# First 256 tokens multiplied before their row factors are known, and their scaled parts written again later

## The chip, the cores and the metric

The kernel runs on one core of a Trainium2 chip. The metric is device time in microseconds (us) of one launch, as a median over several runs. The engines are PE (TensorE, matrix products, with PEld for its weight loads), DVE (VectorE), ACT (ScalarE), POOL (GpSimd) and SP (SyncE, which here only issues DMA transfers). PE accumulates in PSUM, everything else lies in SBUF or in DRAM.

## What is computed

Two sequences of 512 tokens go through one encoder layer. Only its beginning matters here:

```python
def rms_norm(x, g):
    xf = x.astype(jnp.float32)
    y = xf * lax.rsqrt(jnp.mean(xf * xf, axis=-1, keepdims=True) + EPS)
    return (y * g.astype(jnp.float32)).astype(x.dtype)
...
h = rms_norm(x, ln1)
proj = h @ w_in
q, k, v, u, g_att, g_ssm = jnp.split(proj, IN_SPLITS, axis=-1)
...
dt = jnp.exp(log_dt.astype(jnp.float32))[..., None]
mag = jnp.exp(lr * dt)
ang = li * dt
```

Each token's row is divided by its root mean square (the row factor) and multiplied by the gain `ln1` of each column; then come the projections. `u` feeds a state-space branch whose coefficients need `dt`, `mag`, `ang` and powers of the complex number they make. Since a row factor is one number per token, it may as well be applied behind the product: (f x) W = f (x W).

## The kernel before

**Products.** The tokens stand in columns: `xT` is x turned, in eight pieces (k = 0 to 7) of 128 model columns. A float32 product is made of three of a shorter type: each operand is split into a high part (`hi`, a cast on ACT) and a low part (`lo`, what the cast left over, a subtraction on DVE or POOL), and PE adds hi*hi, hi*lo and lo*hi (in code p = 0, 1 and 2, where p == 2 takes the low part of the weights and p == 1 that of the tokens). `hT[s]` holds the two parts of the normalized, turned tokens of sequence s (in the profile `act` for s = 0, `hT` for s = 1). They are used by all projections.

**The opening.** It is written out by hand: PE, ACT, DVE and SP take their instructions in the order of the code there; POOL's order is the scheduler's. The first three columns of `u` (128 outputs each; weights `uw` for c = 0, 1 and `c_hi`, `c_lo` for c = 2) are multiplied while the inputs arrive:

- SP issues row blocks 0 to 3 of `x` (`xt`, 128 tokens x 1024, 512 KB each), then the columns of `xT` (`xc`, 512 tokens, 256 KB each) and the weights in halves of 256 KB, then rows and columns of sequence 2, then small things. A buffer that is used again holds its transfer back until its readers are done, and all transfers behind it.
- `row_root(t)`: ACT squares a row block and sums along the row (L355), POOL adds EPS and takes the power -1/2 (L357, L358).
- `spread(s, t)`: DVE puts the 128 factors on a diagonal (L348), PE multiplies it by ones (L349), so that a PSUM bank holds the factors of the tokens along its columns, the same in every partition.
- `scaled(s, k)`: DVE multiplies a column by gain and factor (L364, `rn_xn`), ACT casts it (L365), DVE or POOL subtracts (L368, L367; POOL for odd k).
- L383 is a warm-up of PE, on row block 2 and ones. L463 are the products, nine for each k (three columns, three parts), 512 tokens wide, first of sequence 1 into `tps`, `tps`, `sps`, then of sequence 2 into `sps`, `acc`, `po`.
- `exp_exact`, an exponential of 15 small DVE instructions on 128x64, runs twice at the very start (L326 to L338), for `dt` and `mag`; the angle follows in pieces during sequence 2.

**Behind it** `u_steps(3)` and `u_steps(4)` are queued in `fill` as 16 steps of three products each (L115 to L117), which `run(n)` puts between the other work; they use the parts of both sequences. Meanwhile DVE makes the powers of the complex number (`pr`, `pi`: `first_power`, L413 to L418, then L479 to L484), ACT copies them (L489 to L493), and DVE makes coefficients (L537 to L549) and tables (L561 to L573: `bpre` and `ctab`, for 16 quads of groups in turn). `bpre` has one buffer: PE's turns (L596) of one quad need its `bpre`, and DVE starts the next quad's `bpre` when they are done. Later a scan over chunks runs on DVE, beside products on PE.

Of the kernel before, what the change touches and what calls it, by code (L numbers as in the profile page):

```python
# [18 lines left out]
P = 128  # L19
D = 1024  # L20
# [43 lines left out]
def hybrid_layer(ctx, tc, x, xT, rel, onehot, early, w_qkv, w_ug, q_gain, k_gain, sink,  # L64
# [165 lines left out]
    def u_steps(c):  # L230
        up, ps = [], {}

        def out(s):
            S.copy(up[0][:, :, s, :], ps[s].rearrange("p (k t) -> p t k", t=T))
            if s:
                u_store(c, up[0])

        def step(s, k):
            if s + k == 0:
                up.append(evp.tile([P, T, NSEQ, NCHUNK], F32, tag="ev", name="up"))  # L240
# [3 lines left out]
            if k == KT - 1:  # L244
                act_owed.append(lambda: out(s))
                if s:
# [25 lines left out]
    with tc.tile_pool(name="xin", bufs=2, reuse_waits="tile") as xin, tc.tile_pool(name="ssmc", bufs=1) as sc:  # L272
# [10 lines left out]
        rows, columns, first_w = {}, {}, []  # L283

        def x_rows(s):
            for t in range(s * 4, s * 4 + 4):
                rows[t] = xin.tile([P, D], F32, tag="xt", name="xt", bufs=4)
                SP.dma_start(rows[t], x[t * P:(t + 1) * P, :])

        def x_columns(s, k0=0, k1=KT):  # L290
            for k in range(k0, k1):
                columns[s, k] = xin.tile([P, HALF], F32, tag="xc", name="xc", bufs=8)
                SP.dma_start(columns[s, k], xT[k, :, s * HALF:(s + 1) * HALF])
# [19 lines left out]
        second = cast_owed[:]  # L313
        del cast_owed[:]
        bc_tiles = {0: b_and_c(0)}
        SP.dma_start(dd[32:48, :], d_skip)
        SP.dma_start(bglu_sb, b_glu)
# [5 lines left out]
        def exp_exact(dst, src):  # L323

            n, r, q = c64("ex_n"), c64("ex_r"), c64("ex_q")
            V.tensor_scalar(r, src, -87.0, 88.5, op0=ALU.max, op1=ALU.min)  # L326
            V.tensor_scalar(n, r, 1.0 / math.log(2.0), ROUND_MAGIC, op0=ALU.mult, op1=ALU.add)
            V.tensor_scalar_add(n, n, -ROUND_MAGIC)
            V.scalar_tensor_tensor(r, n, -LN2_HI, r, op0=ALU.mult, op1=ALU.add)
            V.scalar_tensor_tensor(r, n, -LN2_LO, r, op0=ALU.mult, op1=ALU.add)  # L330
            V.tensor_scalar(q, r, 1.0 / 5040.0, 1.0 / 720.0, op0=ALU.mult, op1=ALU.add)
            V.tensor_mul(q, q, r)
            for cf in (1.0 / 120.0, 1.0 / 24.0, 1.0 / 6.0, 0.5, 1.0):
                V.scalar_tensor_tensor(q, q, cf, r, op0=ALU.add, op1=ALU.mult)
            V.tensor_scalar_add(q, q, 1.0)
            bits = sc.tile([P, GROUPS], I32, tag="ex_i", name="ex_i")
            V.tensor_scalar(bits, n, 127.0, 8388608.0, op0=ALU.add, op1=ALU.mult)
            V.tensor_mul(dst, q, bits.bitcast(F32))  # L338
# [3 lines left out]

        def spread(s, t):

            if t == 0:
                spread_ps[s] = acc()
# [4 lines left out]
        def row_root(t):  # L351

            junk = xin.tile([P, D], F32, tag="rn_junk", name="rn_junk", bufs=1)
            ss = small.tile([P, 1], F32, tag="ss", name="ss")
            S.activation(junk, rows[t], AF.Square, scale=D ** -0.5, accum_out=ss)  # L355
# [4 lines left out]
        def scaled(s, k):  # L360

            xn = xin.tile([P, HALF], F32, tag="rn_xn", name="rn_xn", bufs=3)
            hi, lo = [q[:, k, :] for q in hT[s]]
            V.scalar_tensor_tensor(xn, columns[s, k], ln1_sb[:, k:k + 1], spread_ps[s], op0=ALU.mult, op1=ALU.mult)  # L364
# [5 lines left out]
        def weight_half(raw, w, i):  # L370
            sl = slice(i * KT // 2, (i + 1) * KT // 2)
            S.copy(w[0][:, sl, :], raw[:, sl, :])
            return lambda: V.tensor_sub(w[1][:, sl, :], raw[:, sl, :], w[0][:, sl, :].bitcast(F32))

        exp_exact(dt, ldt)
        for t in range(4):
            row_root(t)
        w_los = [weight_half(raw, w, 0) for raw, w in first_w]
        V.tensor_mul(mag, lr, dt)
        exp_exact(mag, mag)  # L380
        warm = acc()
        for i in range(6):
            PE.matmul(warm[:, 0:P], rows[2][:, 0:P], ones, start=True, stop=True)  # L383

        for t in range(4):
            spread(0, t)
        w_los.pop(0)()
        owed = [scaled(0, 0)]
        second.pop(0)()
        w_los.append(dve_owed.pop())  # L390
# [4 lines left out]
        def u_out(c, s):  # L395
            S.copy(ups[c][:, :, s, :], out_ps[c, s].rearrange("p (k t) -> p t k", t=T))

        def angles():
            yield lambda: V.tensor_mul(ang, li, dt)
# [5 lines left out]
            yield lambda: None  # L405
# [1736 lines left out]
```

## Time and profile before

| | us |
|---|---|
| median of 3 runs | 1452.25 (1452.12 to 1452.64) |
| the profiled execution | 1451.68 |
| its span, first to last instruction | 1449.9 |
| PE busy in the span | 1431.1 (99%) |
| DVE, ACT, POOL busy | 1083.6, 770.8, 190.9 |

How to read its lines: those of the page's fifth part and of the groups give line, engine, operation, output<-inputs, shapes and count, then busy us and mean ns, then idle time ahead and what ended it. Those of a timeline give the start, the us from start to end (of several merged ones where x2 and more stands), and the same names. Matmul records overlap: a 128x512 product has 0.39 us in them, but the next starts 0.227 us later. Those of windows give the busy us of PE, PEld, DVE, ACT and POOL in a stretch, PE's granted clock, the DMA share and GB/s.

### The profile page before, as it was taken

What the parts mean: (1) busy time and instruction counts of PE and PEld (TensorE: products, weight loads), DVE (VectorE), ACT (ScalarE), POOL (GpSimd) and SP (SyncE); (2) the same over time, 40 slices, a digit from 0 to 9 for tenths busy, and PEclk for the clock granted to TensorE, in tenths of its full rate; (3) what the DMA queues carried; (4) which work ended last, traced back from release to release, by engine and by line L of the source; (5) the groups of instructions that cost most, each with busy time, mean ns of one, the idle gap of its engine ahead of it and who ended that gap; (6) DMA issues with size and microseconds to landing.
All of it is one profiled execution on the core that took longest, in us unless ns stands there. A gap on an engine that the chain in (4) does not pass through costs nothing.

```text
span 1449.9 us, 21455 instructions
## 1 busy us (share of the span) xinstructions
PE 1431.1 (99%) x7718; PEld 1225.6 (85%) x7718; DVE 1083.6 (75%) x1842; ACT 770.8 (53%) x1393; POOL 190.9 (13%) x267
## 2 busy tenths in 40 slices
PE   6999999999999999999999999999999999999998
PEld 5888888888999999988888888888888888888887
DVE  7899979974536999987764798777776588475644
ACT  5589962224426999896432455554555444333332
POOL 4111120000222555372001000000000000000000
PEclk9999999999999999999999999999999999999999
DMA  8355568259941433455862335544443994464341
GB/s 304 112 162 173 169 195 284 95 172 287 297 131 44 128 100 110 135 190 167 269 215 95 107 103 188 183 143 141 152 149 121 327 343 127 155 194 144 127 131 58
DMA packets 130134, 243.86 MB, mean 168 GB/s; under 512 B 16059, under 2 KB 59323, under 8 KB 130028
## 3 DMA queue, kind: packets, MB, share of 16 engines
q1 hardware_dynamic: 105740, 187.39, 41.2%
q10 hardware_dynamic: 21888, 46.15, 8.4%
q0 software_dynamic: 2400, 8.95, 1.8%
q8 instruction: 61, 1.00, 0.3%
q14 instruction: 45, 0.37, 0.1%
HBM read 173.20 MB, written 81.82 MB: 176 GB/s over the span
## 4 chain that ended last, share of the span: by engine, by line
PE 94%; DVE 2%; DMA 1%; ACT 1%; issue 1%; POOL 1%; SPq 0%; DVEq 0%; ACTq 0%
PE bank L115 14%; PE bank L117 14%; PE bank L116 14%; PE acc L141 12%; PE acc L732 9%; PE acc L770 5%; PE acc L115 3%; PE acc L117 3%; PE acc L116 3%; PE po L1103 3%; PE sps L1071 2%; PE tps L1087 2%; PE sps L605 2%; PE sps L877 2%; PE lag L620 1%; PE tps L596 1%
## 5 line engine op out<-in xcount | busy, mean ns | idle before, releaser
L117 PE MATMUL bank<-b_hi,a_lo 128*128 128x512 f32 x440 | 171.2, 389 | 0.0
L116 PE MATMUL bank<-b_lo,a_hi 128*128 128x512 f32 x440 | 171.2, 389 | 0.0
L115 PE MATMUL bank<-b_hi,a_hi 128*128 128x512 f32 x440 | 171.2, 389 | 0.0
L2015 ACT CAST a_hi<-d_a 128x1024 fp32r<-128x1024 f32 x55 | 57.8, 1051 | 178.7 <-PE bank L116 175.5
L2016 DVE TENSOR_TENSOR a_lo<-d_a,a_hi 128x1024 fp32r<-128x1024 f32 x55 | 67.4, 1225 | 98.8 <-ACT a_hi L2015 96.7
L117 PE MATMUL bank<-act,u_lo 128*128 128x512 f32 x256 | 99.6, 389 | 0.0
L116 PE MATMUL bank<-act,u_hi 128*128 128x512 f32 x256 | 99.6, 389 | 0.0
L115 PE MATMUL bank<-act,u_hi 128*128 128x512 f32 x256 | 99.6, 389 | 0.0
L117 PEld LDWEIGHTS bank<-b_hi,a_lo 128*128 128x128 f32 x440 | 82.6, 188 | 17.3
L116 PEld LDWEIGHTS bank<-b_lo,a_hi 128*128 128x128 f32 x440 | 82.6, 188 | 17.2
L115 PEld LDWEIGHTS bank<-b_hi,a_hi 128*128 128x128 f32 x440 | 82.6, 188 | 17.0
L732 PE MATMUL acc<-w_hi,hT 128*128 128x256 f32 x384 | 84.4, 293 | 0.0
L732 PE MATMUL acc<-w_hi,act 128*128 128x256 f32 x384 | 81.2, 290 | 0.0
L141 PE MATMUL acc<-act,c_hi 128*128 128x512 f32 x256 | 80.6, 395 | 0.0
L141 PE MATMUL acc<-hT,c_hi 128*128 128x512 f32 x256 | 80.5, 394 | 0.0
L1081 ACT ACTIVATE p<-p,nmx 128x257 f32<-128x257 f32 (+1 forms) x128 | 72.0, 564 | 13.0 <-DVE nmx L1075 12.3
L1075 DVE CUSTOM_DVE_ANT_0 p<-sps,bias,nsink 128x256 f32<-128x256 f32 (+1 forms) x128 | 69.3, 542 | 4.4 <-PE sps L1071 3.0
L1799 ACT CAST u_hi<-s 128x512 fp32r<-128x512 f32 x64 | 39.3, 621 | 59.6 <-PE bank L116 36.2
L2016 DVE TENSOR_TENSOR b_lo<-k,b_hi 128x1024 fp32r<-128x1024 f32 x55 | 67.1, 1220 | 0.0
L732 PEld LDWEIGHTS acc<-w_hi,hT 128*128 128x128 f32 x384 | 63.8, 190 | 0.9
L732 PEld LDWEIGHTS acc<-w_hi,act 128*128 128x128 f32 x384 | 63.1, 190 | 0.8
L1096 DVE TENSOR_TENSOR pl<-tps,ph 128x512 fp32r<-128x512 f32 x80 | 55.0, 688 | 4.5 <-ACT ph L1091 2.7
(407 smaller groups left out, 3939.0 us busy)
## 6 DMA issues: line engine op xcount, KB each, us to landing
d_a<-a_scr SPq DMA_DIRECT2D x55, 512.0 KB, 3.6
u_raw<-in_w_up_dram SPq DMA_DIRECT2D x32, 512.0 KB, 5.8
a_scr<-t ACTq DMA_DIRECT2D x64, 256.0 KB, 2.1
k<-in_w_down_dram SPq DMA_DIRECT2D x32, 512.0 KB, 6.1
a_scr<-a ACTq DMA_DIRECT2D x48, 256.0 KB, 3.3
c_raw<-in_w_ug_dram SPq DMA_DIRECT2D x44, 256.0 KB, 3.5
ct_scr<-ctab SPq DMA_DIRECT2D x16, 576.0 KB, 3.3
ctab_in<-ct_scr SPq DMA_DIRECT2D x32, 288.0 KB, 4.8
```

Of the source, the lines that this page charges most:

```text
L115: PE.matmul(ps, a[0], b[0], start=first, stop=False)
L116: PE.matmul(ps, a[0], b[1], start=False, stop=False)
L117: PE.matmul(ps, a[1], b[0], start=False, stop=last)
L141: PE.matmul(self.ps[s], self.w[p == 2][:, k, :], hT[s][p == 1][:, k, :], start=i % (3 * KT) == 0, stop=i % (3 * KT) == 3 * KT - 1)
L732: PE.matmul(ps, act[p == 2][:, k, col:col + P], self.w[k // 4][p == 1][:, k % 4, :], start=i == 0, stop=i == 3 * KT - 1)
L770: PE.matmul(self.ps[s], w_g[self.m][p == 2][:, k, :], y_part(s, int(p == 1), k), start=k + p == 0, stop=k == KT - 1 and p == 2)
L1075: V.tensor_tensor_reduce(self.p[:, h, 1:1 + self.nk], self.s[h][:, 0:self.nk], biases[self.j][h][:, b0:b0 + self.nk], -1.0, nsink[:, hh:hh ...
L1081: S.activation(p, p, AF.Exp, bias=self.nmx[:, h:h + 1], scale=-1.0, accum_out=self.sums[:, h, self.qb:self.qb + 1])
L1096: V.tensor_sub(pl, self.pt[i], self.hl[i][0].bitcast(F32))
L1103: PE.matmul(self.po, vv, self.hl[i][part], start=i + part == 0, stop=i == self.nkb - 1 and part == 1)
L2015: S.copy(hi, src)
L2016: V.tensor_sub(lo, src, hi.bitcast(F32))
```

## The change

Only the opening is changed; all instructions from the power tables on are the same, on each engine in the same order.

- The first 256 tokens of sequence 1 are split without their factors: `raw_parts` (ACT: gain times column, as it is cast; DVE: gain times column less the high part). Their products, 256 wide, start with the first columns and weights. The factor is applied when the PSUM bank is evacuated: `u_scaled_out` multiplies by `factor` on DVE (three times, during sequence 2).
- The other 256 tokens are scaled as before, 256 wide, in a second pass over k. Of the row blocks, 2 and 3 are therefore loaded first, 4 to 7 then, and 0 and 1 last.
- The parts of the first 256 tokens are needed with their factors by every later product. Their columns are loaded once more (`x_again`, 1 MB) and `rewrite(k)` writes the parts anew; `u_steps(3)` takes sequence 2 first.
- The two exponentials are dealt out, one to three instructions at a time (`some`), over the opening. The warm-up multiplies ones by ones. The squares overwrite their rows instead of a junk tile. `column_in(3)` moves ahead.

**PE, the first products.** Before (L383 is the warm-up, L349 the spreads of the factors, L463 the products; `act_113` and `act_114` are the high and the low parts of sequence 1):

```order
L383 MATMUL acc<-ones,xt 128x128 x6
L349 MATMUL acc<-rs_diag,ones 128x128 x4
L463 MATMUL tps<-act_113,uw_hi 128x512 x2
L463 MATMUL sps<-act_113,c_hi 128x512
L463 MATMUL tps<-act_113,uw_lo 128x512 x2
```

Now, on the same engine (L465 is the warm-up, L443 the products):

```order
L465 MATMUL acc<-ones 128x128 x6
L443 MATMUL tps<-act_113,uw_hi 128x256
L443 MATMUL tps<-act_114,uw_hi 128x256
L443 MATMUL tps<-act_113,uw_lo 128x256
L443 MATMUL tps<-act_113,uw_hi 128x256
```

The spreads have gone from the front; two of them now stand ahead of the second 256 tokens, four among that part's last products, and two in sequence 2.

**ACT, the second 256 tokens** (L417 are the casts of the scaled columns, L400 the squares of row blocks 4 to 7). Now:

```order
L417 CAST act_113<-rn_xn 128x256 x3
L400 ACTIVATE xt,ss<-xt 128x1024
L417 CAST act_113<-rn_xn 128x256
L400 ACTIVATE xt,ss<-xt 128x1024
L417 CAST act_113<-rn_xn 128x256
L400 ACTIVATE xt,ss<-xt 128x1024
L417 CAST act_113<-rn_xn 128x256
L400 ACTIVATE xt,ss<-xt 128x1024
L417 CAST act_113<-rn_xn 128x256 x2
```

A square of a row block stands ahead of each cast from k = 3 on; before they stood so among the casts of k = 4 to 7 of all 512 tokens.

**DVE, ahead of the power tables.** Before (L221 is the low part of weights, L418 the first power's last instruction, L479 the first of the tables):

```order
L221 TENSOR_TENSOR c_lo<-c_raw,c_hi 128x512
L413 MEMSET pr 128x64
L414 MEMSET pi 128x64
L415 TENSOR_TENSOR sh<-sh 128x64
L416 TENSOR_SCALAR sh<-sh 128x64
L417 TENSOR_TENSOR pr<-mag,sh 128x64
L418 TENSOR_TENSOR pi<-mag,sn 128x64
L479 TENSOR_TENSOR tm_640<-pr 128x64
```

Now, between the same first power and the same first table (L415 and L420 are the columns written anew and their low parts):

```order
L459 TENSOR_TENSOR pi<-mag,sn 128x64
L221 TENSOR_TENSOR c_lo<-c_raw,c_hi 128x512
L415 SCALAR_TENSOR_TENSOR rn_xn<-xa,early_sb,acc 128x256 x3
L420 TENSOR_TENSOR act_114<-rn_xn,act_113 128x256
L1018 TENSOR_SCALAR nsink<-nsink 128x16
L415 SCALAR_TENSOR_TENSOR rn_xn<-xa,early_sb,acc 128x256 x2
L420 TENSOR_TENSOR act_114<-rn_xn,act_113 128x256
L415 SCALAR_TENSOR_TENSOR rn_xn<-xa,early_sb,acc 128x256 x2
L420 TENSOR_TENSOR act_114<-rn_xn,act_113 128x256
L415 SCALAR_TENSOR_TENSOR rn_xn<-xa,early_sb,acc 128x256
L420 TENSOR_TENSOR act_114<-rn_xn,act_113 128x256
L566 TENSOR_TENSOR tm_769<-pr 128x64
```

Twelve instructions have come in ahead of the power tables. The other four low parts are POOL's.

The diff, cut to what the text speaks of:

```diff
-    def u_steps(c):
+    def u_steps(c, order=(0, 1)):
...
-        return [lambda s=s, k=k: step(s, k) for s in range(NSEQ) for k in range(KT)]
+        return [lambda s=s, k=k: step(s, k) for s in order for k in range(KT)]
...
-        x_rows(0)
-        x_columns(0, 0, 1)
+        x_half(0, 0)
         first_weights(0)
-        column_in(2)
-        x_columns(0, 1, 4)
+        third_weights(0)
+        for k in range(1, 4):
+            x_half(k, 0)
+        x_row(2)
         first_weights(1)
-        x_columns(0, 4, KT)
-        x_rows(1)
-        x_columns(1)
+        third_weights(1)
+        for k in range(4, KT):
+            x_half(k, 0)
+        x_row(3)
+        for k in range(KT):
+            x_half(k, 1)
+        for t in range(4, 8):
+            x_row(t)
+        for k in range(4):
+            x_column(k)
+        for t in range(2):
+            x_row(t)
+        for k in range(4, KT):
+            x_column(k)
         bc_tiles = {0: b_and_c(0)}
         SP.dma_start(dd[32:48, :], d_skip)
+        column_in(3)
+        for i in range(2):
+            x_again(i)
...
+        def raw_parts(k):
+            hi, lo = [q[:, k, 0:H2] for q in hT[0]]
+            src, gain = columns[0, k][:, 0:H2], ln1_sb[:, k:k + 1]
+            S.activation(hi, src, AF.Copy, scale=gain)
+            return lambda: V.scalar_tensor_tensor(lo, src, gain, hi.bitcast(F32), op0=ALU.mult, op1=ALU.subtract)
...
+        def u_scaled_out(c):
+            V.tensor_tensor(ups[c][:, :, 0, 0:H2 // T], out_ps[c, 0][:, 0:H2].rearrange("p (k t) -> p t k", t=T),
+                            factor.rearrange("p (k t) -> p t k", t=T), op=ALU.mult)
...
+        in_turn = {0: ((1, 2), (1, 2)), 1: ((3, KT), (3,)), 2: ((KT + 1, 4), (KT, 4)), 3: ((KT + 2, 5), (KT + 1, KT + 2)),
+                   4: ((6,), (5,)), 5: ((7,), (6,)), 6: ((), (7,)), 7: ((), ())}
+        for k in range(KT):
+            if k == 1:
+                halves(3)
+                row_root(2)
+                halves(KT)
+            else:
+                halves(*in_turn[k][0])
+            if k == 5:
+                row_root(3)
+            low_parts(*in_turn[k][1])
+            if k > 3:
+                some(3)
+            u_products(0, k, 0, H2, by_part if k else by_column)
+        for t in (2, 3):
+            spread(0, t)
+        low = scaled(0, 0, H2, HALF)
+        for k in range(KT):
+            after = scaled(0, k + 1, H2, HALF) if k + 1 < KT else None
+            low()
+            low = after
+            if 0 < k < 5:
+                row_root(k + 3)
+            some(1)
+            u_products(0, k, H2, HALF, by_part, slice(0, 6 if k == KT - 1 else 9))
...
+            if k == 2:
+                for t in range(2):
+                    spread(0, t)
+                factor = xin.tile([P, H2], F32, name="factor", bufs=1)
+                S.copy(factor, spread_ps[0][:, 0:H2])
         column_in(4)
-        fill += u_steps(3)
+        fill += u_steps(3, (1, 0))
         fill += u_steps(4)
         run(2)
-        for c in range(3):
-            u_out(c, 1)
-            u_store(c, ups[c])
+        for k in range(2, KT):
+            rewrite(k)
+            rewritten.pop(0)()
+            if k < 5:
+                u_out(k - 2, 1)
+                u_store(k - 2, ups[k - 2])
+        for fn in rewritten:
+            fn()
```

More of the change, by code (lines that the diff above doesn't have):

```diff
@@ L338, in exp_exact @@
-            V.tensor_mul(dst, q, bits.bitcast(F32))
+            yield lambda: V.tensor_scalar(bits, n, 127.0, 8388608.0, op0=ALU.add, op1=ALU.mult)
+            yield lambda: V.tensor_mul(dst, q, bits.bitcast(F32))
         dt, mag, ang, kk = c64("dt"), c64("mag"), c64("ang"), c64("kk")
         spread_ps, root = {}, {}
-        def spread(s, t):
-            if t == 0:
-                spread_ps[s] = acc()
-            dg = xin.tile([P, P], F32, tag="rs_diag", name="rs_diag", bufs=4)
-            V.tensor_scalar_mul(dg, ident, root[s * 4 + t])
-            PE.matmul(spread_ps[s][:, t * P:(t + 1) * P], ones, dg, start=True, stop=True)
@@ L351, in row_root @@
[L351 to L355, printed above, removed]
-            root[t] = small.tile([P, 1], F32, tag="rs", name="rs")
-            GP.tensor_scalar_add(ss, ss, EPS)
-            GP.tensor_tensor(root[t], ss, neg_half[:, 0:1], op=ALU.pow)
[L360 to L364, printed above, removed]
-            S.copy(hi, xn)
-            if k % 2:
-                return lambda: GP.tensor_tensor(lo, xn, hi.bitcast(F32), op=ALU.subtract)
-            return lambda: V.tensor_sub(lo, xn, hi.bitcast(F32))
@@ L370, in weight_half @@
[L370 to L390, printed above, removed]
-        u_w = [w for raw, w in first_w] + [weights[2]]
-        out_ps = {}
-        ups = [xin.tile([P, T, NSEQ, NCHUNK], F32, tag="up", name="up", bufs=3) for c in range(3)]
-        def u_out(c, s):
-            S.copy(ups[c][:, :, s, :], out_ps[c, s].rearrange("p (k t) -> p t k", t=T))
         def angles():
+            yield from exp_exact(dt, ldt)
@@ L404, in angles, with some, spread @@
             yield lambda: V.tensor_scalar(ang, ang, -3.1415925, 3.1415925, op0=ALU.max, op1=ALU.min)
-            yield lambda: None
         small_ops = angles()
+        def some(n):
+            for _ in range(n):
+                next(small_ops, nop)()
+        def spread(s, t):
+            dg = xin.tile([P, P], F32, tag="rs_diag", name="rs_diag", bufs=4)
+            V.tensor_scalar_mul(dg, ident, root[s * 4 + t])
+            PE.matmul(spread_ps[s][:, t * P:(t + 1) * P], ones, dg, start=True, stop=True)
@@ L465, in hybrid_layer, with halves @@
-        for fn in w_los:
-            fn()
+        warm = acc()
+        spread_ps[1] = acc()
+        spread_ps[0] = acc()
+        for i in range(6):
+            PE.matmul(warm[:, 0:P], ones, ones, start=True, stop=True)
+        for c in range(3):
+            out_ps[c, 0] = (tps, tps, sps)[c]()
+        some(4)
+        raw_parts(0)()
+        for c in range(3):
+            weight_half(c, 0)()
+        lo = {}
+        def halves(*names):
+            for n in names:
+                lo[n] = raw_parts(n) if n < KT else weight_half(n - KT, 1)
@@ new lines, in hybrid_layer, with rewrite @@
+        low = scaled(1, 0)
+        for c in range(3):
+            out_ps[c, 1] = (sps, acc, lambda: ps_o.tile([P, 512], F32, tag="po", name="po"))[c]()
+        rewritten = []
+        def rewrite(k):
+            rewritten.append(scaled(0, k, 0, H2, columns["again", k]))
+        for k in range(KT):
+            after = scaled(1, k + 1) if k + 1 < KT else None
+            low()
+            low = after
+            if k < 3:
+                u_out(k, 0, H2, HALF)
+            if k < 2:
+                row_root(k)
+            if k in (3, 4, 5):
+                u_scaled_out(k - 3)
+            some(3)
+            if k == 4:
+                S.activation(sn, ang, AF.Sin)
+                S.activation(sh, ang, AF.Sin, scale=0.5)
+            if k == 6:
+                first_power()
+            if k in (3, 5):
+                pay(cast_owed, 1)
+            if k in (4, 6):
+                pay(dve_owed)
+            if k > 5:
+                rewrite(k - 6)
+            u_products(1, k, 0, HALF, by_part)
+            if k == 2:
[3 more added lines that the diff above has]
+                S.copy(factor, spread_ps[0][:, 0:H2])
```

145 lines of the change are left out of this document (77 added, 68 removed).

## Prediction

> **What bounds the kernel now.** I read the page first, then the waits of PE (TensorE), then the timelines of the opening. The page's first lines, its slices and its chain:
>
> ```profile
> span 1449.9 us, 21455 instructions
> PE 1431.1 (99%) x7718; PEld 1225.6 (85%) x7718; DVE 1083.6 (75%) x1842; ACT 770.8 (53%) x1393; POOL 190.9 (13%) x267
> PE   6999999999999999999999999999999999999998
> PE 94%; DVE 2%; DMA 1%; ACT 1%; issue 1%; POOL 1%; SPq 0%; DVEq 0%; ACTq 0%
> ```
>
> PE is busy everywhere but in the first slice of 36 us, so a change in the opening pays what it takes from PE's idle time there, if PE's head start lives through the stages behind. PE's waits and its timeline (start, us, what; the product of interest is L463):
>
> ```profile
> PE acc L383 <- DVE ex_q L331: 8.0, 1, 8.0
> PE tps L463 <- ACT act L365: 1.5, 1, 1.5
> PE acc L349 <- DVE rs_diag L348: 1.2, 2, 0.7
> PE sps L463 <- DVE c_lo L221: 0.7, 1, 0.7
> 8.04 2.90 PE L383 MATMUL acc<-ones,xt 128*128 128x128 f32 x12 [8.04 <-DVE ex_q L331]
> 14.13 0.73 PE L463 MATMUL tps<-act,uw_hi 128*128 128x512 f32 x2 [1.49 <-ACT act L365]
> 27.95 0.60 PE L349 MATMUL acc<-rs_diag,ones 128*128 128x128 f32 x4
> 34.72 0.39 PE L463 MATMUL sps<-hT,uw_hi 128*128 128x512 f32 x1
> 51.04 0.39 PE L115 MATMUL acc<-act,c_hi 128*128 128x512 f32 x1
> ```
>
> The first product starts at 14.13, the second sequence's first at 34.72, and the next stage at 51.04. The second sequence (72 products, 16.3 us) has no gap, so all that can be won lies before 34.72, where 72 products of 0.227 us (51.04 - 34.72 over 72) need only 16.3 us.
>
> **The first product.** The loads land in the order of issue, one behind another:
>
> ```profile
> 2.73 0.20 DVE L326 TENSOR_SCALAR ex_r<-early_sb 128x64 f32<-128x64 f32 x1 [0.91 <-DMA early_sb<-in_early_dram]
> 5.35 1.06 ACT L355 ACTIVATE rn_junk<-xt 128x1024 f32<-128x1024 f32 x1 [3.35 <-DMA xt<-in_x_dram]
> 6.69 1.06 ACT L355 ACTIVATE rn_junk<-xt 128x1024 f32<-128x1024 f32 x1 [0.19 <-DMA xt<-in_x_dram]
> ```
>
> 512 KB are there at 5.35, the next 512 KB 1.3 us later. Now 384 KB stand ahead of the first product (half a column of x, half a weight column): 5.35 less a quarter of 1.3, so 5.0, and a weight cast of 0.62 (below) makes **5.7**. Bounds: 4.5, if short loads land as the first small one did (read at 2.73); 6.0, if 384 KB take as long as 512 KB did.
>
> **First half of sequence 1 (256 tokens).** Of products on 256 columns the trace has this stretch, first and last row of nine products (ends left out), and of the other operations these rows (mean ns behind the bar):
>
> ```profile
> 371.97 0.40 PE L732 MATMUL acc<-w_hi,act 128*128 128x256 f32 x2
> ...
> 372.92 0.28 PE L732 MATMUL acc<-w_lo,act 128*128 128x256 f32 x1
> L364 DVE SCALAR_TENSOR_TENSOR rn_xn<-xc,early_sb,acc 128x512 f32<-128x512 f32 x16 | 11.6, 738 | 1.1 <-PE acc L349 0.9 <-DMA xc<-in_xT_dram 0.2
> L372 ACT CAST uw_hi<-uw_raw 128x512 fp32r<-128x512 f32 x4 | 2.5, 618 | 1.1 <-DMA uw_raw<-in_w_ug_dram 0.9
> L373 DVE TENSOR_TENSOR uw_lo<-uw_raw,uw_hi 128x512 fp32r<-128x512 f32 x4 | 2.7, 682 | 0.0
> L367 POOL TENSOR_TENSOR hT<-rn_xn,hT 128x512 fp32r<-128x512 f32 x4 | 5.2, 1309 | 10.4 <-ACT hT L365 10.4
> L358 POOL TENSOR_TENSOR rs<-ss,neg_half 128x1 f32<-128x1 f32 x8 | 4.6, 569 | 0.7
> L334 DVE SCALAR_TENSOR_TENSOR ex_q<-ex_q,ex_r 128x64 f32<-128x64 f32 x10 | 2.3, 225 | 0.3
> L355 ACT ACTIVATION_READ_ACCUMULATOR rn_junk<-xt 128x1 f32 x8 | 1.5, 186 | 0.0
> L357 POOL TENSOR_SCALAR ss<-ss 128x1 f32<-128x1 f32 x8 | 2.7, 332 | 8.1 <-DVE mag L379 5.3 <-ACT rn_junk L355 2.6
> L512 ACT COPY a8s<-pr 128x256 f32<-128x256 f32 x1 | 0.4, 405 | 0.0
> L479 DVE TENSOR_TENSOR tm<-pr 128x256 f32<-128x256 f32 x1 | 0.4, 427 | 0.0
> ```
>
> Eight products start between 371.97 and 372.92: 0.119 us each, so 72 take 8.6 us (two halves cost 0.8 us more than 16.3). PE would end at 14.3, but k = 4 needs the second weight halves. Ahead of the last of them 2.5 MB are queued (row block 2 among them): 5.35 + 4 x 1.3 = 10.5. Its cast (0.62) and subtraction (0.68), with the other two subtractions and k = 4's own low part on DVE, put it at about 12.9; the 30 products behind it take 3.6 us: **16.7**. The exponentials' small steps (225 ns each, twelve between here and the diagonals) fill DVE so that the diagonals come some 0.4 us after PE is done.
>
> **The factors for the second half.** Two diagonals and spreads (1.0 us with that wait), then the scaled column and its cast, 256 wide. The trace has neither; they lie between half and all of 738 and 618 ns, and I take 0.46 and 0.41, by the two 128x256 rows. First product of the second half: **18.6**.
>
> **Second half.** 8.6 us of products and four spreads (1.0). ACT has eight casts (0.41) and four squares (1.06 and a readout of 0.19): 8.3 us. POOL has four subtractions and four roots: at 0.7 each (half of 1309; bounds 0.65 and 1.31) and 0.33 + 0.57, 6.4 us. Neither is longer than PE, but they are in line: a cast stands behind the square of its turn, a subtraction behind a root. I put 1.3 us of waits for that (nothing if they run ahead, 3 us at POOL's upper bound). End **29.7**; then 0.74 and 0.62 for the first column of sequence 2: **31.1**, 3.6 us before 34.72.
>
> **Sequence 2** is as before, but for the two spreads of the early tokens (0.5 us on PE) and a subtraction on POOL that comes 0.2 us late. The next stage starts 2.9 us earlier than 51.04. I take off 0.3 us for PE's slow start: the warm-up's twelve records took 2.90 us, four of the spreads at 27.95 only 0.60 us: 0.21 us apart (2.90 less the last one's 0.4, over twelve) and 0.11 (0.60 less 0.27, over three). The same 128x128 operation costs half as much once PE has run for a while. The warm-up now waits for a memset alone, ends near 3.7 and leaves PE idle until 5.7. At half speed, 0.21 apart, the 36 products up to k = 3 would end at 13.3, against the weights' 12.9: 0.4 us if it lasts so long, nothing if it ends sooner. **PE's head start: 2.6 us.**
>
> [...]
>
> **What DVE, ACT and DMA do with it.** The parts written anew add eight columns to DVE and ACT just ahead of the power tables:
>
> ```profile
> 44.41 0.11 DVE L413 MEMSET pr<- 128x64 f32 x1
> 46.22 0.22 DVE L479 TENSOR_TENSOR tm<-pr 128x64 f32<-128x64 f32 x1
> 51.28 0.42 DVE L484 TENSOR_TENSOR pi<-tm,tm 128x256 f32<-128x256 f32 x1
> 53.27 0.63 ACT L489 COPY e<-pr 64x512 f32<-64x512 f32 x1
> 68.70 1.29 DVE L221 TENSOR_TENSOR c_lo<-c_raw,c_hi 128x512 fp32r<-128x512 f32 x2 [0.81 <-ACT c_hi L220]
> 73.88 1.23 DVE L561 TENSOR_TENSOR bpre<-b,bk 128x1024 f32<-128x1024 f32 x1 [3.89 <-PE tps L596]
> 85.50 1.23 DVE L573 TENSOR_TENSOR bpre<-bpre,tb 128x1024 f32<-128x1024 f32 x1
> 89.05 1.03 PE L596 MATMUL tps<-ident,bpre 128*128 128x128 f32 x8
> 40.00:45.00 5.00, 5.00 (x24) 4.14 (x23) 4.01 (x9) 3.86 (x7) 2.05 (x2) 1.00 0.17 52
> ```
>
> In sequence 2 DVE waits for the factor: PE has the spreads at 31.1 + 6.1 + 0.5, ACT copies it by 38.4; all of DVE's queue stands behind (the columns from k = 5 on, the evacuations), which brings the memset of pr to about 44.7 (44.41 before): the exponentials' steps here and the three scaled evacuations eat DVE's part of the head start. Then come eight columns (0.39 apart), four subtractions (0.35), and some 1.6 us of waits for ACT's casts and POOL: 6.2 us. The power tables end at about 58 instead of 51.7. ACT's copies start right then, not 1.6 us after as before (53.27), so they are 4.9 us late, and with them the tables of the first quad. DVE's idle 0.81 and 3.89 us take up 4.7 of that. So DVE starts the second quad's bpre at 73.9 plus 0 to 1 us; I take **0.5 us later than now**, where PE is 2.6 us earlier. The bounds are 1.5 us later (POOL's and DVE's upper ends) and 0.8 us earlier (all at half of the 512-wide rows).
>
> From 73.88 on DVE has hardly a gap, and PE's third turn at 89.05 comes 2.3 us after its bpre (85.50 + 1.23). So PE keeps at most 2.3 - 0.5 = **1.8 us**, and waits 0.8 us there. Behind that both run as before, the same instructions in the same order, and PE's slices show no room to lose or win it.
>
> At no cost: the junk tile that goes (same squares), the columns read again (1 MB, landing near 35, at the 0.17 DMA share of 40:45), and SP's queue. There the loads of row blocks 0 and 1 wait for squares 4 and 5 (near 22) and hold four columns of sequence 2, b and c, column 3 and the columns read again behind them; the first of these is read after 36. Without that cover each us late would be one on PE.
>
> **Sum.** The profiled execution took 1451.68 us (span 1449.9 and 1.8 around it) and would take 1449.9; it lies 0.6 under the median of 1452.25, so the median becomes **1450.4**.
>
> **Rivals.**
> - *DVE keeps up.* If 256 columns cost half of 512, the rewriting is 1.3 us shorter, bpre is not late and PE keeps 2.6 to 3.5 us: 1448.7 to 1449.7. Against it speak the rows at 427 and 405, two thirds of the 512-wide ones; for it, that my 1.6 us of waits are the softest term. 0.25.
> - *PE stays at half clock* through the first half, since it keeps stopping for weights: k = 4 to 7 then cost 36 x 0.09 = 3.2 us more, with the 0.4 above 3.6, less the 0.3 counted: PE is 0.7 us late, 1453.0. It decides if products after 13 us are still over 0.2 us apart. Half of that is as likely: 1451.3 to 1453.0, 0.13. [...]
> - *The tables come late* (slower). If the casts, which stand in ACT's line with the evacuations, and POOL's subtractions at 1.3 us string the rewriting out, each us beyond 2.3 us of DVE's delay is one on the total; the point is bpre of the second quad after 76.2. At POOL's upper bound DVE is 2.4 us late: 1452.4; with the casts waiting as well some 5: 1455. 0.12.
> - *The loads don't get there sooner*, since 128 KB cost as much as 256 KB (0.65 us): four of them stand ahead of the second weight halves (1.3 us), all sixteen ahead of row block 7, 5 us, which outruns its square by 2: PE keeps some 0.6 us, 1451.7. 0.05.
>
> **How the numbers follow.** The forecast (1449.7 to 1451.3) has 0.45. The range leaves out the far ends of the first and third rival: **1448.7 to 1453.0**. 0.2% (2.9 us) is what a measurement of this kernel can tell from no change: faster by more, under 1449.35, is three fifths of the first rival, 0.15; slower by more is the worse half of the third, 0.06; within it 0.79.
>
> **What would show it.** First product at 5.7 (wrong over 7); first half done near 16.7, second near 29.7; sequence 2 from 31.1; the L115 products behind it 2.6 us earlier; the power tables done near 58; a new wait of PE for bpre near 87. No wait there and a time under 1449.5 would mean that DVE was taken too slow; products over 0.2 us apart after 13 us would mean the clock.

## The result, and the profile after

The changed kernel is slower: 1467.15 us median of 5 runs (1464.74 to 1468.89), the kernel before 1452.43 us in the same comparison (5 runs, 1452.12 to 1452.64). The ratio is 1.0105, with a 95% interval of 1.0094 to 1.0116: 14.7 us. The forecast was 1450.4 (1448.7 to 1453.0). The profiled execution, the slowest of the five, took 1468.89 us with a span of 1467.1. Lines behind the front are 87 higher than before (a L1783 is now L1870).

The head of the page, PE's slices and the chain, of the kernel after:

```profile
span 1467.1 us, 21659 instructions
PE 1440.5 (98%) x7790; PEld 1233.6 (84%) x7790; DVE 1089.6 (74%) x1865; ACT 777.1 (53%) x1410; POOL 191.3 (13%) x271
PE   8999999999999999999999979999999999999998
PE 89%; DVE 5%; DMA 2%; issue 2%; ACT 1%; POOL 1%; SPq 0%; DVEq 0%; ACTq 0%; POOLq 0%
```

There are two new things here. The first slice is an 8 where it was a 6, so the front did get denser. But the 24th slice (843 to 880 us) is a 7 where it was a 9, some 800 us behind the last edited line. PE's waits of the kernel after (what waited, for whom: us in total, times, longest) name it:

```profile
PE bank L115 <- DVE a L1870: 7.4, 1, 7.4
PE acc L117 <- DVE c_lo L221: 2.2, 2, 1.7
PE sps L692 <- ACT bm L685: 2.1, 3, 1.5
PE tps L443 <- ACT uw_hi L426: 2.0, 1, 2.0
PE sps L443 <- ACT hT L417: 1.7, 2, 1.1
...
PE tps L443 <- ACT act L417: 1.0, 1, 1.0
...
PE acc L395 <- DVE rs_diag L394: 0.7, 1, 0.7
```

The last four lie in the front, the first three behind it, and those three had no counterpart of that size before. Five rows of PE's timeline before, at the places that matter, and then the same places after (start, us, what, idle time ahead and its end):

```profile
62.38 0.39 PE L117 MATMUL acc<-act,c_lo 128*128 128x512 f32 x1
...
74.15 0.39 PE L117 MATMUL acc<-act,c_lo 128*128 128x512 f32 x1
...
83.88 0.38 PE L605 MATMUL sps<-u_sb,bm 128*128 128x128 f32 x2
...
847.34 0.39 PE L115 MATMUL bank<-act,u_hi 128*128 128x512 f32 x1
...
1190.28 0.39 PE L116 MATMUL bank<-b_lo,a_hi 128*128 128x512 f32 x1
```

```profile
6.05 0.79 PE L443 MATMUL tps<-act,uw_hi 128*128 128x256 f32 x2 [2.05 <-ACT uw_hi L426]
...
18.18 0.28 PE L443 MATMUL sps<-act,c_hi 128*128 128x256 f32 x1
...
20.12 0.51 PE L443 MATMUL tps<-act,uw_hi 128*128 128x256 f32 x2 [1.01 <-ACT act L417]
...
31.86 0.50 PE L443 MATMUL sps<-hT,uw_hi 128*128 128x512 f32 x1 [1.14 <-ACT hT L417]
...
50.60 0.39 PE L115 MATMUL acc<-hT,c_hi 128*128 128x512 f32 x1
...
62.60 0.50 PE L117 MATMUL acc<-act,c_lo 128*128 128x512 f32 x1 [0.51 <-DVE c_lo L221]
...
76.41 0.50 PE L117 MATMUL acc<-act,c_lo 128*128 128x512 f32 x1 [1.73 <-DVE c_lo L221]
...
87.98 0.71 PE L692 MATMUL sps<-u_sb,bm 128*128 128x128 f32 x4 [1.54 <-ACT bm L685]
...
861.29 0.77 PE L115 MATMUL bank<-act,u_hi 128*128 128x512 f32 x1 [7.44 <-DVE a L1870]
...
1207.33 0.50 PE L116 MATMUL bank<-b_lo,a_hi 128*128 128x512 f32 x1 [0.92 <-DVE b_lo L2103]
```

Subtracting the two gives where the time went. PE is 0.44 us ahead at the start of the next stage (50.60 against 51.04), 0.22 behind at 62, 2.26 at 76, 4.10 at 88, 13.95 at the first `bank` product and 17.05 near 1207, of 17.2 us between the two spans. (That is 2.5 us more than the 14.7 between the medians: the profiled execution of after lies 1.7 us over its median, that of before 0.75 under its own.) Between 88 and 861 come another 2.4 us besides the 7.44, and between 861 and 1207 three more. Of these, 0.92 is the wait at 1207, which no other profile here has, and 1.6 us near 343 and some 1.7 behind 861 are time at half clock, as the windows of after show (stretch, then busy time of PE, PEld, DVE, ACT and POOL, the granted clock, the DMA share):

```profile
340.00:345.00 5.00, 3.41 (x17) 2.73 (x16) 3.21 (x5) 3.57 (x8) 0.00 (x0) 0.81 0.53 143
345.00:350.00 5.00, 5.00 (x27) 4.25 (x26) 3.28 (x5) 1.41 (x3) 0.00 (x0) 0.85 0.98 334
...
855.00:860.00 5.00, 0.00 (x0) 0.00 (x0) 4.92 (x9) 4.37 (x9) 0.00 (x0) 0.85 0.14 52
860.00:865.00 5.00, 3.71 (x9) 2.96 (x10) 3.55 (x6) 2.37 (x4) 0.00 (x0) 0.50 0.25 57
```

### The profile page after: what moved, and what is told of

It is laid out like the page before. It is cut to its first block, busy times and chain, and to the rows that moved or that the text cites. A ratio compares the mean times of both kernels' runs of the same rounds, so it can differ in the third digit from the quotient of the medians.

```text
span 1467.1 us, 21659 instructions
## 1 busy us (share of the span) xinstructions
PE 1440.5 (98%) x7790; PEld 1233.6 (84%) x7790; DVE 1089.6 (74%) x1865; ACT 777.1 (53%) x1410; POOL 191.3 (13%) x271
## 3 DMA queue, kind: packets, MB, share of 16 engines
q10 hardware_dynamic: 21888, 46.15, 8.3%
## 4 chain that ended last, share of the span: by engine, by line
PE 89%; DVE 5%; DMA 2%; issue 2%; ACT 1%; POOL 1%; SPq 0%; DVEq 0%; ACTq 0%; POOLq 0%
PE bank L116 13%; PE bank L115 13%; PE bank L117 13%; PE acc L141 11%; PE acc L819 9%; PE acc L857 5%; PE po L1190 3%; PE acc L115 3%; PE acc L117 2%; PE acc L116 2%; PE sps L1158 2%; PE tps L1174 2%; PE sps L692 2%; PE sps L964 2%; PE lag L707 1%
## 5 line engine op out<-in xcount | busy, mean ns | idle before, releaser
L115 PEld LDWEIGHTS bank<-act,u_hi 128*128 128x128 f32 x256 | 48.6, 190 | 18.0 <-ACT f_hi L1759 7.8
```

The lines of the kernel that those rows point to most:

```text
L115: PE.matmul(ps, a[0], b[0], start=first, stop=False)
```

## The experiments

Two theories were put beside each other. **Bank:** the wait at 861 is a PSUM bank that isn't free, and only the place of the tiles has changed. **Late DVE:** DVE trails PE from the front on, and 861 is where it shows. DVE's order around 861 made the first the likelier. These two rows are the wait's releaser before and after:

```profile
854.09 0.68 DVE L1783 TENSOR_TENSOR a<-acc,u 128x512 f32<-128x512 f32 x1
```

```profile
860.46 0.69 DVE L1870 TENSOR_TENSOR a<-acc,u 128x512 f32<-128x512 f32 x1
```

The same addition stands 6.75 us behind the first `bank` product before (854.09 against 847.34), and nobody waited for it. It reads the last accumulator tile. The built programs give the banks of the last three accumulators and of the first tiles of the pool that follows them:

```
before   p1 (0): bank 0   p1 (1): bank 2   p2 (1): bank 1   then bank tiles: 0 7 6 1 2 5 3 4
after    p1 (0): bank 2   p1 (1): bank 1   p2 (1): bank 0   then bank tiles: 0 7 6 1 2 5 3 4
```

After the change the first `bank` tile takes the bank of the tile that is read last. All comparisons below stand against the kernel before in the same run of the chip (medians 1450.94 to 1451.63 there):

| kernel | median us | minus before |
|---|---|---|
| after (its own comparison, before 1452.43) | 1467.15 | +14.7 |
| a_bank | 1457.24 | +5.6 |
| b_bank | 1461.52 | +9.9 |
| a_mid | 1464.75 | +13.4 |
| a_norw | 1452.79 | +1.2 |
| a_bank_warm | 1459.59 | +8.0 |
| a_bank_exp | 1456.45 | +5.5 |
| a_bank_pool | 1458.07 | +7.1 |
| a_bank_load | 1455.38 | +4.4 |
| a_best | 1453.96 | +3.0 |
| a_bank_order | 1454.20 | +2.8 |
| a_fix | 1450.94 | -0.4 |

Single runs of one variant (4 to 11 of each) spread over 1 to 6 us, against 0.5 to 2.4 for the kernel before, so that differences of about 1 us between two of them are not more than a hint.

### The rotation of the banks: a_bank, b_bank, a_mid

```diff
# a_bank: the kernel after with
         for i in range(6):
+            if i in (2, 4):
+                warm = acc()
             PE.matmul(warm[:, 0:P], ones, ones, start=True, stop=True)
# b_bank: the kernel before, and a_mid: the kernel after, each with
+            if i == 3:
+                warm = acc()
```

> After, with the six warm-up products on three accumulator tiles in turn instead of one: no instruction more or less, but every later accumulator tile moves round the three banks by two, so that the first bank tile of the next program part gets the bank whose last reader ran as early as in the kernel before. Theory (the wait of 7.44 us at 861.29 is a PSUM bank whose reader a L1870 was queued late on DVE, and the 2 us at half clock behind it follow from that idle time): 7.4 to 9.5 us less than 1467.2, so 1457.7 to 1459.8, no gap over 0.3 us at the first bank product. Rival (DVE is late by then against PE, whatever the bank): the wait stays or moves by some products, 1465 to 1468.

> Before, with its six warm-up products on two accumulator tiles: no instruction more or less, the rotation of the accumulator banks shifted to that of the kernel after; nothing of the change in it. Theory: the same wait appears at the first bank product, about 7 us, with some 2 us at half clock behind it: 1459.5 to 1462 against 1452.4. Rival (the wait comes from the change's late DVE): 1452.0 to 1453.0.

> After, with the six warm-up products on two accumulator tiles: the third position of the rotation, in which the first bank tile of the next part gets the bank that ACT's copy u L1862 reads last (857.97 to 858.55 in the profile of after, 4.9 us behind the last product before it), neither the early nor the latest reader. Theory: a wait of about 4.9 us there instead of 7.44 or none, then some time at half clock: 1462 to 1465.5. Rival (any shift that keeps accumulators to the end waits for DVE's a L1870): as after, 1465 to 1468.

Two lines that add no work to any engine (the page of a_bank counts two instructions more than that of after, the waits of PE for the two further tiles) took 9.1 us off the excess of the changed kernel (14.7 to 5.6), and one swap of the same kind added 9.9 us to the kernel before (ratio 1.0066, 1.0052 to 1.008). The last three accumulators lie in banks 0, 2 and 1 in a_bank, as in before, in 2, 1 and 0 in b_bank, as in after, and in 1, 0 and 2 in a_mid. The first `bank` product in a_bank, b_bank and a_mid:

```profile
853.65 0.39 PE L115 MATMUL bank<-act,u_hi 128*128 128x512 f32 x1
```

```profile
854.36 0.77 PE L115 MATMUL bank<-act,u_hi 128*128 128x512 f32 x1 [7.42 <-DVE a L1785]
854.92 0.63 PE L116 MATMUL bank<-act,u_hi 128*128 128x512 f32 x1
```

```profile
859.20 0.73 PE L115 MATMUL bank<-act,u_hi 128*128 128x512 f32 x1 [4.75 <-ACT u L1864]
```

In b_bank, without one line of the change, the wait of after is there to 0.02 us. In a_mid the bank's last reader is ACT's copy, and the wait is 4.75 us (4.9 was expected). So the three positions of the rotation cost 0, 4.75 and 7.4 us, and the rival with its late DVE falls. The half clock belongs to it: the products behind the wait in b_bank last 0.63 us instead of 0.39, and the granted clock is 0.50 from 855 to 860. (The total of a_mid lies only 1.3 us under that of after, for a wait 2.7 us shorter; the runs of after alone spread over 4 us.)

### The parts written anew: a_norw

```diff
-            rewritten.append(scaled(0, k, 0, H2, columns["again", k]))
+            rewritten.append(lambda: None)
```

> After, without the parts written anew (eight columns of DVE and ACT work and four POOL subtractions left out; the fourth column and those behind it then multiply the first 256 tokens unscaled). Without them the spread's accumulator tile is not held so long, and the rotation is that of the kernel before. Theory (rotation, and DVE late by the rewriting): the wait at the first bank product goes, and the stalls of PE near 62.6, 76.4 and 88.0 (0.51, 1.73, 1.54 us) go but for 0.5 us; the power tables end near 55.7 instead of 61.95; 1452 to 1455. Rival for the second half (DVE is late by the dealt-out exponentials, not by the rewriting): the stalls keep 2 us or more, 1456 to 1458.

1452.79, 1.2 us over before. PE has no stall over 0.2 us between 48 and 120, and the power tables end at 55.9 (forecast 55.7). The wait at the first `bank` product is gone. Of a_norw:

```profile
847.66 0.39 PE L115 MATMUL bank<-act,u_hi 128*128 128x512 f32 x1
```

The rotation went back to that of before without any other edit: the built program has its last three accumulators in banks 0, 2 and 1. That shows what had shifted it: in after the parts written anew read the spread's accumulator until 55.6, so the accumulators behind it are dealt out to the other banks first.

What the rewriting costs behind the front can be read with less noise than in the totals, as PE's time from the first product of the next stage to its fourth turn: 46.15 us in before (51.04 to 97.19) and in a_norw, 50.81 in after (50.60 to 101.41) and 50.69 in a_bank (49.65 in a_bank_warm, with the same work: some 1 us hangs on a landing, as shown below). That is 4.5 us between a_bank and a_norw, as between their totals (4.4).

### The clock in the first half: a_bank_warm

```diff
-        for i in range(6):
+        for i in range(14):
```

> As a_bank, with fourteen warm-up products instead of six, so that PE runs from 1.07 to about 6 without idle time. If half clock in the first half (products 0.213 us apart from 6.05 to 11.9, some 2.5 us) is what made the first half end at 18.5 instead of 16.7: products 0.12 apart from the first, and the first half ends 1 to 2 us sooner. If the second weight halves set it (low parts on DVE ready at 14.42): the same end within 0.4 us, PE waits for them instead, and the total is that of a_bank within 0.7 us. I expect the second.

This diff and those behind it are against a_bank. The first product starts at 6.43, the products run 0.12 us apart wherever their parts are there (steadily from 8.2 to 11.3; in after only from 12.1), and PE then waits instead, 1.24 us at 12.83 for a column's part. The low part of the third weight column's second half still comes last, and the last product of the first half starts where it did in after (18.23 against 18.18). Of a_bank_warm, and then of after:

```profile
14.55 0.39 PE L443 MATMUL sps<-act,c_lo 128*128 128x256 f32 x1 [0.22 <-DVE c_lo L427]
...
18.23 0.28 PE L443 MATMUL sps<-act,c_hi 128*128 128x256 f32 x1
```

```profile
14.48 0.38 PE L443 MATMUL sps<-act,c_lo 128*128 128x256 f32 x1 [0.21 <-DVE c_lo L427]
```

In both, PE waits for that low part near 14.5 and then runs without a wait to the end of the first half, so in after the slow products (0.21 us apart up to 12.05) cost the first half nothing; its loads did. (In after the granted clock reads 1.00 from 6 to 14, where products are 0.21 us apart and where they are 0.12 apart: the spacing is what the profile shows of half clock here. The comparison is with after and not with a_bank, whose profile has this low part only at 15.76, behind a late load.) This holds for this order of loads alone: in a_bank_load, below, the same low part is ready at 13.37, PE comes to it only at 13.92, without a wait, and there the slow products set the end. The total came out 2.3 us above a_bank's (1455.39 to 1460.64 in four runs; the granted clock is 1.000 in the fastest, which is the profiled one, and 0.996 in the two slowest). That wasn't expected and isn't explained.

### What keeps DVE late: a_bank_exp, a_bank_pool, a_bank_order

```diff
# a_bank_exp
-        some(4)
+        some(12)
         raw_parts(0)()
# a_bank_pool
-            if k % 2:
+            if k % 2 or src is not None:
                 return lambda: GP.tensor_tensor(lo, xn, hi.bitcast(F32), op=ALU.subtract)
# a_bank_order
-            def tables(q):
+            def tables(q, between=None):
...
                 complex_table(bpre, q, b2, b_s, bk, bb[:, 0], T)
+                if between:
+                    between()
...
-            tables(0)
+            tables(0, lambda: (pay(cast_owed), pay(dve_owed)))
             run(4)
             pay(act_owed)
-            pay(cast_owed)
-            pay(dve_owed)
```

> As a_bank (1457.2), with twelve instead of four of the exponentials' steps ahead of the first column's parts, where DVE is idle from 3.6 to 5.5 us. Theory (DVE is late at the power tables because the dealt-out steps stand between the columns of sequence 2, where DVE has no gap from 38 to 47): eight steps fewer there, the memset of pr 1.5 to 3 us earlier than in the profile of after against the start of sequence 2, the stalls near 64, 78 and 89 together 1 to 2.5 us instead of 3.7, 1455 to 1456.3. Rival (DVE waits there for the factor, ACT and PE, and the eight columns written anew alone make it late): 1456.5 to 1458.

> As a_bank, with all eight subtractions of the parts written anew on POOL instead of every second one: DVE has four instructions of 0.42 us fewer ahead of the power tables, POOL 6.4 us instead of 3.2. If DVE's length sets the stalls, the power tables come 1.4 to 1.7 us sooner and the total 1 to 1.7 us: 1455.5 to 1456.3. If the columns there wait for a buffer that POOL gives back (three buffers), nothing or a loss: 1456.8 to 1459.

> As a_bank (1457.2), with the fifth column's casts and low parts (c_hi, c_lo of column 5) put between the first quad's bpre and its ctab tables instead of behind both; nothing left out or added. Theory (the stalls near 78 and 89 are one delay: DVE has 13.8 us of work from c_lo of column 4 to c_lo of column 5, PE 12.1; the late c_lo also gives its raw buffers back late, so that the next column's load and ACT's cast of it come late and ACT's copy of bm behind them): both go, the stall near 64 (0.5 us) stays, 1453.5 to 1455. Rival (DVE is late as a whole, so that the order within it only moves the wait to the tables): a wait of PE for bpre or ctab of like size, 1456 to 1458.

a_bank_exp took the stall near 62 away but left the two behind it at 1.74 and 1.49 us; +5.5 against +5.6 is the rival's number, though its profile, unlike a_bank's, has half clock near 343 (granted clock 0.999 over the profiled run, 1.000 in a_bank). From the first product of the next stage to the fourth turn PE takes 50.20 us, 0.5 less than in a_bank.

a_bank_pool's total gained nothing either (+7.1), as the second case of its expectation said, but its profile shows a small gain: from the first column written anew to the first power table DVE takes 5.0 us (50.24 to 55.20) instead of a_bank's 6.1, less than the four subtractions left out, since its columns now wait for POOL 1.2 us in four places (a_bank: 0.6 us in one). Half of that gain is lost again in the power tables, which take 6.6 us instead of 6.0: while POOL's subtractions run, small operations that take 0.22 us elsewhere take up to 0.77 (they took 0.21, 0.21 and 0.67 in after, with half as many subtractions there). The stall near 62 went, and 1.69 us stayed behind it. DVE in a_bank_pool, and then POOL:

```profile
52.01 0.48 DVE L415 SCALAR_TENSOR_TENSOR rn_xn<-xa,early_sb,acc 128x256 f32<-128x256 f32 x1 [0.51 <-POOL act L419]
...
55.47 0.77 DVE L569 TENSOR_TENSOR tm<-pi 128x64 f32<-128x64 f32 x1
56.28 0.67 DVE L570 TENSOR_TENSOR pr<-tm,tm 128x64 f32<-128x64 f32 x1
56.98 0.23 DVE L571 TENSOR_TENSOR tm<-pr,pi 128x64 f32<-128x64 f32 x1
```

```profile
55.41 0.75 POOL L419 TENSOR_TENSOR act<-rn_xn,act 128x256 fp32r<-128x256 f32 x1
...
56.10 0.76 POOL L419 TENSOR_TENSOR act<-rn_xn,act 128x256 fp32r<-128x256 f32 x1
```

In these rows the two slow operations of DVE end just behind POOL's subtractions: these at 56.16 and 56.86, DVE's at 56.24 and 56.95. The same profile has a stretch at granted clock 0.65 and 0.67 from 340 to 350, so its total doesn't measure the edit alone.

a_bank_order only swaps two things in DVE's and ACT's queues, and took 2.8 us (+5.6 to +2.8, inside its forecast); from the first product of the next stage to the fourth turn PE takes 47.59 us instead of 50.69. The stalls of 1.74 and 1.43 us of a_bank are gone; 0.55 us stays at 63 and 0.41 at 90. In a_bank_order the fifth column's low part now ends before PE needs it:

```profile
72.92 0.69 DVE L221 TENSOR_TENSOR c_lo<-c_raw,c_hi 128x512 fp32r<-128x512 f32 x1
...
75.08 0.39 PE L117 MATMUL acc<-act,c_lo 128*128 128x512 f32 x1
```

These rows of after show the mechanism:

```profile
47.39 0.11 DVE L454 MEMSET pr<- 128x64 f32 x1
...
61.52 0.43 DVE L571 TENSOR_TENSOR pi<-tm,tm 128x256 f32<-128x256 f32 x1
61.86 1.29 DVE L221 TENSOR_TENSOR c_lo<-c_raw,c_hi 128x512 fp32r<-128x512 f32 x2
...
75.67 1.29 DVE L221 TENSOR_TENSOR c_lo<-c_raw,c_hi 128x512 fp32r<-128x512 f32 x2
76.87 1.22 DVE L648 TENSOR_TENSOR bpre<-b,bk 128x1024 f32<-128x1024 f32 x1
```

```profile
79.20 0.62 ACT L220 CAST c_hi<-c_raw 128x512 fp32r<-128x512 f32 x1 [4.26 <-DMA c_raw<-in_w_ug_dram]
81.66 0.62 ACT L220 CAST c_hi<-c_raw 128x512 fp32r<-128x512 f32 x1 [1.85 <-DMA c_raw<-in_w_ug_dram]
```

From one `c_lo` to the next DVE needs 13.81 us (75.67 - 61.86), PE 12.08 (76.41 - 1.73 - 62.60): once PE waits for the first, or meets it just in time, it waits 1.73 for the second. That is why this stall was 1.69 to 1.74 us in all eight profiles with the rewriting and the old order (after, a_mid, a_bank, a_bank_warm, a_bank_exp, a_bank_pool, a_bank_load and a_best), however early the front ended. And what reads the raw column late gives its buffer back late: the next column lands late, ACT stands at its cast (79.20, 81.66) with `bm` in its queue behind, and PE waits 1.54 for `bm` at 87.98. How much of this last wait there is depends on the landing: in a_bank_warm, where the second cast starts at 80.60, it is 0.35 us, and in a_bank_pool 0.35 as well.

### The front itself: a_bank_load, a_best, a_fix

```diff
# a_bank_load
         for k in range(1, 4):
             x_half(k, 0)
-        x_row(2)
         first_weights(1)
         third_weights(1)
         for k in range(4, KT):
             x_half(k, 0)
+        x_row(2)
         x_row(3)
...
-            if k == 1:
-                halves(3)
-                row_root(2)
-                halves(KT)
-            else:
-                halves(*in_turn[k][0])
+            halves(*in_turn[k][0])
             if k == 5:
+                row_root(2)
                 row_root(3)
# a_best: a_bank_exp, a_bank_pool and a_bank_load, and both edits below;
# a_fix: a_bank_order, a_bank_exp and a_bank_load, and both
+        early = small.tile([P, 1], F32, tag="ss", name="ss")
+        S.activation(early, neg_half[:, 0:1], AF.Copy, scale=1.0)
...
-        for i in range(6):
+        for i in range(10):
```

> As a_bank, with the load of row block 2 (512 KB) issued behind the second weight halves and the columns' first halves instead of ahead of them, and its square just ahead of row block 3's. Theory (the first half ends at 18.5 and not at 16.7 because the second weight halves land 1.3 us or more later than forecast): they land 1.3 to 1.9 us sooner, the first half ends 1.3 to 1.9 us sooner; the second half starts 0.5 to 1.5 us sooner, as the two squares then stand in line, and with it everything up to the power tables: 1455.7 to 1456.7. Rival (the low parts' line on DVE sets it): first half as before within 0.5 us, 1456.7 to 1457.7.

> As a_bank, with the three edits of a_bank_exp, a_bank_pool and a_bank_load together, an activation of one column at the start (ACT's table load of 1.28 us, which stood at 3.68 between the first column's landing and its cast, is then done before), and ten warm-up products. First product near 5.0 instead of 6.05; sequence 2 from about 29.5; power tables near 57; stalls behind the front together below 1 us. If DVE's lateness and the loads are what the front lost: 1449.5 to 1452.5, that is within 0.2% of before or a little under it. If a further bound stands behind them: 1453 to 1456.

> As a_bank_order, with the edits of a_bank_exp and a_bank_load, the early activation and the ten warm-up products (all of a_best but the subtractions on POOL). First product near 5.3, sequence 2 from 30.5, no stall of PE over 0.5 us between 48 and 120, and PE's head start of about 2 us kept: 1448.5 to 1451 against before's 1451 on this chip. If PE still waits for DVE behind 48: 1452 to 1454.

a_bank_load started the second half at 19.26 (20.12 in after, 21.51 in a_bank) and took 1.2 us off the excess, about as expected, in spite of the squares that then stand in line; by the spread of single runs this total is a hint. a_best, at +3.0, missed the hoped-for range and fell into that of a further bound behind the front: its front reached the second sequence at 30.56, but the 1.74 and 1.39 us behind it were still there, and that is what pointed to a_bank_order. With that in it, a_fix is level with before: ratio 1.0, 95% interval 0.9992 to 1.0009. Three places of a_fix:

```profile
5.27 0.38 PE L445 MATMUL tps<-act,uw_hi 128*128 128x256 f32 x1
...
48.74 0.39 PE L115 MATMUL acc<-hT,c_hi 128*128 128x512 f32 x1
...
336.50 0.49 PE L962 MATMUL sps<-u_sb,toep 128*128 128x128 f32 x2 [1.31 <-ACT ysb L972]
```

The next stage starts at 48.74, 2.3 us before 51.04, nearly the head start that was forecast. It is not kept, so that the time lies within the range expected of a_fix but not for the reason given there: 0.39 us go to a wait for `bpre` at 87.6, and at 336.5 PE waits 1.31 us for `ysb` where it waited 0.5 before; the rest goes in pieces that no single wait names. The first `bank` product starts at 847.30, against 847.34 before. The wait for `ysb` was between none (b_bank) and 1.77 us (a_bank_pool) in the profiles here, in no relation to PE's lead; what sets it was not tried.

## Why the prediction was wrong, point by point

**The step that failed most** is the one sentence on everything behind the front: "Behind that both run as before, the same instructions in the same order, and PE's slices show no room to lose or win it." The instructions and their order are the same. Their PSUM banks are not. The prediction followed every tile that the change makes, but not what holding one of them longer does to those that are dealt out afterwards. It cost 9.1 us (a_bank against after) or 9.9 (b_bank), and was none of the rivals. Without it the forecast would still have failed: a_bank is 5.6 us over before, and the range ended 0.6 over.

**DVE behind the front: right in kind, too small, and looked for at the wrong tile.** The memset of `pr` was put at 44.7 and came at 47.39. The rewriting was right: from 49.81 to 56.0, 6.2 us as forecast. The power tables ended at 61.95 instead of 58, 2.7 of these 4 us lost ahead of the rewriting, the second quad's `bpre` began at 76.87, 3.0 us later than before instead of 0.5. The late-tables rival named 76.2 as the point from which it decides, so it came true, but with another first sufferer: I priced PE's wait for `bpre`, and ahead of `bpre` in DVE's queue stands `c_lo` of the next column, which PE needs sooner. It cost 2.8 us by the totals (a_bank_order); together with the rest of what the rewriting brings, 4.4 (a_norw against a_bank).

**The front: each mark late, and the head start 0.44 us instead of 2.6.** First product 6.05 (5.7): ACT's table load stood between the first column's landing and its cast, and the prediction had no row for it. In after:

```profile
3.68 1.28 ACT L408 ACT_TABLE_LOAD   x1 [3.68 <-DMA xc<-in_xT_dram]
...
12.61 0.60 ACT L426 CAST c_hi<-c_raw 128x512 fp32r<-128x512 f32 x1
```

First half done at 18.5 (16.7), because the last weight half's cast came at 12.61, where its low part was expected to be done at 12.9, and DVE's line put that part at 13.74 to 14.42. Second half from 20.12 (18.6), sequence 2 from 31.86 (31.1), so that the 1.3 us of waits in the second half were a little too many. Two sums of the forecast here are 0.2 us more than their terms (12.9 and 3.6 make 16.5, not 16.7; 18.6, 8.6, 1.0 and 1.3 make 29.5, not 29.7), which is small beside what was missed. Then two stalls in sequence 2 that the forecast put at nothing: 0.67 us for the early tokens' diagonals (DVE took 1.28 us for one of them, from 37.84 to 39.12, beside a subtraction of POOL from 37.77 to 39.04, and 0.28 for the other) and 0.52 for a cast. a_fix shows that most of the 2.6 was to be had: 2.3 with another order of loads, the table load moved, a longer warm-up and the exponentials' steps earlier.

**The rivals.** "PE stays at half clock" was to be decided by the spacing after 13 us: it was 0.12, and a_bank_warm shows that in after the slow products before were covered by the loads. "The loads don't get there sooner" was partly so. "DVE keeps up" fell. The mechanism of the slower side was there, with a third of the loss; the range failed because no rival had a consequence outside the edited stage and those right behind it.

In sum, along the chain from after by a_bank and a_bank_order to a_fix: 9.1 us bank, 2.8 us DVE's order, and 3.2 us for the edits of the front (+2.8 to -0.4; in the two profiles the next stage starts 2.4 us sooner, 48.74 against 51.13). These make 15.1, the 14.7 measured and the 0.4 that a_fix lies under before. They are steps of one chain, so that they must add up; that the bank and DVE's order are causes rests on the traces and on b_bank, not on this sum.

## What to carry to other kernels

A tile that was held longer moved the later tiles of its pool to other buffers here, and where that pool closed and another opened on the same banks, the first new tile inherited the last reader of what lay there (a wait of 0, 4.75 or 7.4 us by the bank alone): compare the banks of the two programs at such seams, not the instructions alone. When an engine's queue grows, ask which of its results is needed first, not which is longest, and move that one ahead; a front that ended sooner left those stalls here as long as they were, and the new order removed them. And a gain of 2 us in the first 3% of a kernel has to pass all the waits behind it: of a_fix's 2.3 us at 48.74, 0.04 are left at the first `bank` product.

## What the runs showed that was not expected

- PE's clock is down behind the long wait, and that costs time of its own: behind 7.4 us of idle time products are 0.43 us apart instead of 0.23, for some 4 us in after (861.3 to 865.3, granted clock 0.50) and 5.6 in b_bank (854.4 to 860.0, granted clock 0.50), and behind 4.75 us in a_mid for 3.5 (859.2 to 862.7).
- After also shows half clock from 343 to 346 (granted clock 0.52) behind two waits of 0.83 and 0.76 us only (341.4 and 342.6), while a_bank had 0.70 and 0.77 there and kept full clock (1.000 over its profiled run). The length of these two waits doesn't decide it: a_bank_warm (1.01 and 0.76), a_bank_order (1.22 and 0.76) and a_fix (1.31 and 0.76) kept full clock too (1.000 over each profiled run). The half clock costs 1.6 us in after. It was in four of the eleven profiles of changed kernels (after, a_mid, a_bank_exp and a_bank_pool, with 0.996, 0.998, 0.999 and 0.998 over the whole run), and it may be why these kernels spread more from run to run than before; that was not tried.
- One load of 512 KB (row block 2) landed at 9.1 us in after and at 11.0 in a_bank, and the loads right behind it 1.3 to 1.5 us later: two executions of the same loads differ by that much, and in the six other profiles with that order it landed between 9.1 and 10.1.
